# Ten of 31 taps of a convolution on GpSimd, split weights for all products, and later sums

## The chip, the cores and the metric

The kernel runs on one NeuronCore of a Trainium2 chip. The metric is the device time of one execution in microseconds, as a median of runs. TensorE (PE) multiplies matrices, VectorE (DVE) and ScalarE (ACT) do elementwise work, GpSimd (POOL) can do some of it, and SyncE (SP) issues the loads. Each engine works through its own queue in order and waits for the others by semaphores.

## The reference

Two transformer-like blocks run one after the other on x of 256 tokens by 1024 features, in fp32. The first has an attention over compressed, selected and windowed keys, a short convolution of 3 taps, and an FFN. The second, to which most of the change belongs, is in short:

```
n = rmsnorm(h) ;  z = n @ w_in                    # c_a, c_g, q, k, v, qi, ki, wi, two gates
u = c_a * sigmoid(c_g)
u = causal_depthwise_conv(u, conv_w[31, 1024]) + conv_b      # y[t] = sum over d of w[30-d] * u[t-d]
y_conv = silu(layernorm(u)) @ w_conv_out
y_attn = attention(q, k, v, top-64 keys by an index of qi, ki, wi) @ w_attn_out
h = h + (g_conv * y_conv + g_attn * y_attn) @ w_mix_out
h = h + cross_attention(rmsnorm(h), rmsnorm(mem))
h = h + relu(rmsnorm(h) @ w_ff1)**2 @ w_ff2 ;  return rmsnorm(h)
```

## The kernel before, in words

Activations lie with features on the 128 partitions and the 256 tokens along the free dimension, in tiles of four groups of features (128 x 4 x 256, fp32, pool "half", 24 buffers, `H4`); a *half* of the 1024 features is one such tile.

Weights come in *units* of 128 x 2048 (1 MB) by DMA from SyncE, in a fixed order (class `Stream`). ScalarE rounds a unit to `wh` (L125, in two pieces of 1024 columns) and VectorE subtracts to get the rest `wl` (L126). A product is then three matmuls, wh·xh, wh·xl and wl·xh (`mm3`, L261 to L263): a unit of the feature-major form (`Feat`) has 16 products of 256 columns, 48 matmuls; a unit of the token-major form (`Tok`) has 8 of 512 columns, 24 matmuls. `W.next()` keeps the splits two units ahead of the unit in use (`AHEAD` = 3). Four units, `NATIVE` = 81, 85, 89 and 97 of the order, are not split: their raw weights are multiplied with the raw activations `xn` (L290, and L343 in the token-major form), where each product of a feature-major unit stands in the profile as two instructions. Unit 81 is the first of q, 85 of k, 89 of v (token-major), 97 of a gate.

TensorE's queue is in the program's order (`MANUAL`); for the other engines a planner orders the instructions by their place in the program and by readiness. Work that goes beside the products is written as generators in a list `side`; `pump()` lets each take one step, up to its next `yield`. A feature-major unit pumps twice and a token-major one twice or more, so a step is about half a unit of TensorE's time. `drain(g)` runs what is left of g at that place.

The generators that the change touches:

- `norm_side` in `ffn_up`: after 5 steps the squares (ScalarE) and their folds (VectorE), two steps later the column sums on TensorE (`col_stats`, L427), then the scale, by a power on GpSimd (L435).
- `attention2`: the index products, eight rounds of top-8 (L1050, L1051), then eight chunks of attention, each: scores (L1069), softmax, four steps later the transposes (`probs_T`, L1000), one step after these the product with v (`heads_pv`, L1010) into the single buffer of the PSUM pool `pso`, which ScalarE and VectorE then empty (L1015, L1016).
- `conv`: for each half, 31 taps d = 0 to 30, with shifted slices of u added into y. Tap 0 is ScalarE's alone (L1113). Of the others four in five are multiplied by ScalarE into a tile `cp`, four instructions (L1118), and added by VectorE in one (L1119); one in five is done by VectorE alone, in four multiply-adds (L1122). `CONV_RATE` = (5, 4) yields four times in five taps. It starts when the first half of u is ready, and must be done before the product with `w_conv_out`.
- `cross`: the cross attention's four products with v alternate between the PSUM pools `pss` and `pso`.

After the second half of the projections (`group(xs2, ...)`) stand q, k, v and the gates, 20 units, and beside these run `conv` and `attention2`.

Of the kernel before, what the change touches and what calls it, by code (L numbers as in the profile page):

```python
# [9 lines left out]
F32 = mybir.dt.float32  # L10
# [6 lines left out]
T = 256  # L17
# [119 lines left out]

RAW_BUFS = 3
LOAD_AHEAD = 2
NATIVE = (81, 85, 89, 97)  # L140
SPLIT_BUFS = 3
AHEAD = 3
H_BUFS = 24
# [4 lines left out]
LAG2 = 4  # L148
# [10 lines left out]
def hybrid_conformer_kernel(ctx, tc, stop, dbg, xT, memT, wall, wtok, wkiwi, wcmp, par_d, cst_d, gfin_d, out):  # L159
# [105 lines left out]
    class Feat:  # L265
# [7 lines left out]
        def chunk(self, c):  # L273
# [10 lines left out]
            def one(kk, o):  # L284
                k = ks[kk]
                sl = slice(o * 128, o * 128 + 128)
                first = c == 0 and kk == 0 and o % 2 == 0
                last = end and kk == 3
                if wl is None:
                    P.matmul(out=ps[o // 2][:, o % 2].rearrange("p (a s) -> p a s", s=2), lhsT=wh[:, kk, sl], rhs=turns(act.raw(k)), start=first, stop=last, skip_group_check=True)  # L290
                else:
                    mm3(ps[o // 2][:, o % 2], wh[:, kk, sl], wl[:, kk, sl], act.hi(k), act.lo(k), first, last)

# [180 lines left out]
    with tc.manual_schedule(engines=MANUAL):  # L474
# [399 lines left out]
        def ffn_up(act, src, tagr, bcast):  # L874
            res = {}

            def norm_side():
                for _ in range(5):
                    yield
                s = sq_sum(src, "s")  # L880
                yield
                yield
                ps = col_stats(s)
                r = rstd_col(ps, D, "r" + tagr)
                r2 = const.tile([128, 2], F32, name="rsq" + tagr)
                V.tensor_tensor(r2, r, r, op=ALU.mult)
                res["col"] = r2
                if not bcast:
                    return
                dg = col_diag(r2)  # L890
                yield
                ps = diag_bcast(dg)
                rb = S([128, T], "rb", 4)
                A.activation(out=rb, in_=ps, func=AF.Copy)
                res["b"] = rb
# [108 lines left out]

        def heads_pv(pt, nb, v, h0, sp, tt, pool=None):

            po = PS() if pool is pss else pso.tile([128, 512], F32, name="o", tag="o")
            for r in range(2):
                for b in range(nb):
                    P.matmul(out=po[:, r * 128:r * 128 + 128], lhsT=v(b, h0 + r), rhs=pt[:, r, b],  # L1010
                             start=(b == 0), stop=(b == nb - 1))
            tk = slice(tt * 128, tt * 128 + 128)
            o = po[:, 0:256].rearrange("p (r t) -> p r t", r=2)
            h, l = sp.hi(h0, 2)[:, :, tk], sp.lo(h0, 2)[:, :, tk]
            A.activation(out=h, in_=o, func=AF.Copy)  # L1015
            V.tensor_sub(l, o, h.bitcast(F32))  # L1016

        def attention2():
# [39 lines left out]
                yield  # L1058
            chunks = [(tt, hp) for hp in range(4) for tt in range(2)]
            live = {}  # L1060
            for n in range(len(chunks) + LAG2 + 1):
                if n < len(chunks):
                    tt, hp = chunks[n]
                    S_ = 128 * (tt + 1)
# [18 lines left out]
                m = n - LAG2  # L1083
                if 0 <= m < len(chunks):
                    live["t", m] = probs_T(live.pop(m), chunks[m][0] + 1)
                m = n - LAG2 - 1
                if m >= 0:
                    tt, hp = chunks[m]
                    heads_pv(live.pop(("t", m)), tt + 1,
# [14 lines left out]
        def conv():  # L1104
            cnt = 0
            for hf in range(2):
                while ("u", hf) not in done:
                    yield
                for d in range(31):
                    w = [par[:, wco + 8 * (30 - d) + 4 * hf + i:wco + 8 * (30 - d) + 4 * hf + i + 1] for i in range(4)]  # L1110
                    if d == 0:
                        for i in range(4):
# [11 lines left out]
                    cnt += 1  # L1124
                    if cnt * CONV_RATE[1] // CONV_RATE[0] != (cnt - 1) * CONV_RATE[1] // CONV_RATE[0]:
                        yield
                if hf == 0:
                    s = H4(name="ys")
                    V.tensor_tensor(s[:, 0:2], y[0][:, 0:2], y[0][:, 2:4], op=ALU.add)
# [154 lines left out]
        def cross():  # L1284
# [24 lines left out]
                if n == 1:  # L1309
                    yield  # L1310
            for n, (tt, hp) in enumerate(chunks):
                heads_pv(live.pop(("t", n)), 2, lambda b, h: vmf[b][:, 128 * h:128 * h + 128], 2 * hp, cs2, tt, pool=pso if n % 2 else pss)

        cr = start(cross())
        pump()
# [181 lines left out]
```

## Time and profile before

| | us |
|---|---|
| median of 3 runs | 923.16 (922.21 to 924.12) |
| profiled execution | 920.19 |
| its span | 918.1 |
| busy: TensorE, VectorE, ScalarE, GpSimd | 897.3, 658.5, 546.0, 16.9 |

The profile is of one execution. Lines such as L126 are those of the kernel's file; `wl<-wr,wh` are the tile that an instruction writes and those that it reads. Times stand in us from the span's start, means in ns. Matmuls are pipelined, so the time of one (some 0.28 us for 256 columns) is longer than its distance to the next, and the distance between starts is what a product costs.

### The profile page before, as it was taken

The page shows a single profiled execution, that of the slowest core. Times are in us where ns is not written, and L with a number is a line of the kernel's source. Part 1 is how long each engine was busy: PE and PEld are TensorE (multiplying, and loading weights), DVE is VectorE, ACT ScalarE, POOL GpSimd, SP SyncE. Part 2 cuts the span into 40 slices and gives each one's busy share as a digit, 9 for nine tenths or more (in the row PEclk, how much of TensorE's full clock was granted, in tenths as well). Part 3 has the DMA queues.
Part 4 walks back from the last instruction along what each step waited for, and adds up shares of the span by engine and source line. Part 5 has one row for each costly group of instructions (what it writes and reads, how often), then busy time and mean ns, then how long its engine had stood idle before and what let it go on. Part 6 is the DMA issues. An engine that isn't in the chain of part 4 may idle for free.

```text
span 918.1 us, 17258 instructions
## 1 busy us (share of the span) xinstructions
PE 897.3 (98%) x7238; PEld 857.1 (93%) x7238; DVE 658.5 (72%) x1033; ACT 546.0 (59%) x921; POOL 16.9 (2%) x21
## 2 busy tenths in 40 slices
PE   8999999999989999999999999999999999999996
PEld 8999988999989999999998879989999899998885
DVE  5578898458666775548699988987787675675542
ACT  7534667444556664435696799977566565654432
POOL 0011000000000000000000000000000000000000
PEclk9999999999999999999999999999999999999999
DMA  8754533455545565553553445344565263555541
GB/s 310 282 176 145 200 108 127 147 214 191 187 145 206 199 229 198 212 187 139 205 186 107 172 175 197 126 151 178 204 254 184 93 233 140 195 191 198 214 138 46
DMA packets 25998, 165.00 MB, mean 180 GB/s; under 512 B 3008, under 2 KB 3648, under 8 KB 7360
## 3 DMA queue, kind: packets, MB, share of 16 engines
q1 hardware_dynamic: 25632, 163.38, 50.0%
q8 instruction: 56, 0.92, 0.4%
q10 hardware_dynamic: 288, 0.52, 0.1%
q14 instruction: 22, 0.18, 0.1%
HBM read 162.58 MB, written 1.05 MB: 178 GB/s over the span
## 4 chain that ended last, share of the span: by engine, by line
PE 87%; DVE 6%; ACT 3%; issue 2%; DMA 1%; POOL 0%; SPq 0%; POOLq 0%; DVEq 0%
PE m L261 22%; PE m L263 22%; PE m L262 22%; PE m L346 4%; PE m L347 4%; PE m L348 4%; PE m L290 3%; DVE wl L126 3%; ACT wh L125 1%; PE s L721 1%; PE m L343 1%; DVE y L1119 1%; DMA wr<-in_wall_dram 1%; PE o L761 1%; PE o L1010 1%
## 5 line engine op out<-in xcount | busy, mean ns | idle before, releaser
L126 DVE TENSOR_TENSOR wl<-wr,wh 128x1024 fp32r<-128x1024 f32 (+2 forms) x298 | 348.8, 1195 | 163.3 <-ACT wh L125 163.0
L125 ACT ACTIVATE wh<-wr 128x1024 fp32r<-128x1024 f32 (+2 forms) x298 | 298.4, 1036 | 216.2 <-PE m L262 122.2
L261 PE MATMUL m<-xh,wh 128*128 128x256 f32 x384 | 108.8, 283 | 0.4 <-ACT wh L125 0.4
L263 PE MATMUL m<-xh,wl 128*128 128x256 f32 x384 | 105.9, 276 | 0.9 <-DVE wl L126 0.9
L261 PE MATMUL m<-xnh,wh 128*128 128x256 f32 x376 | 106.7, 284 | 0.0
L262 PE MATMUL m<-xh,wh 128*128 128x256 f32 x384 | 105.8, 276 | 0.2 <-DVE xh L401 0.2
L262 PE MATMUL m<-xnh,wh 128*128 128x256 f32 x376 | 103.5, 275 | 0.0
L263 PE MATMUL m<-xnh,wl 128*128 128x256 f32 x376 | 103.5, 275 | 0.0
L1118 ACT ACTIVATE cp<-u,par 128x255 f32<-128x255 f32 (+23 forms) x192 | 78.7, 489 | 0.0
L261 PEld LDWEIGHTS m<-xh,wh 128*128 128x128 f32 x384 | 73.7, 192 | 2.2 <-issue 1.4
L263 PEld LDWEIGHTS m<-xh,wl 128*128 128x128 f32 x384 | 73.8, 192 | 1.3 <-DVE wl L126 1.3
L262 PEld LDWEIGHTS m<-xh,wh 128*128 128x128 f32 x384 | 73.8, 192 | 0.4 <-DVE xh L401 0.4
L262 PEld LDWEIGHTS m<-xnh,wh 128*128 128x128 f32 x376 | 72.2, 192 | 0.8 <-issue 0.5
L261 PEld LDWEIGHTS m<-xnh,wh 128*128 128x128 f32 x376 | 72.2, 192 | 0.8 <-issue 0.5
L263 PEld LDWEIGHTS m<-xnh,wl 128*128 128x128 f32 x376 | 72.3, 192 | 0.0
L261 PE MATMUL m<-x5h,wh 128*128 128x256 f32 x256 | 71.7, 280 | 0.0
L261 PE MATMUL m<-fh,wh 128*128 128x256 f32 x256 | 71.5, 279 | 0.0
L263 PE MATMUL m<-x5h,wl 128*128 128x256 f32 x256 | 71.3, 278 | 0.0
L262 PE MATMUL m<-x5h,wh 128*128 128x256 f32 x256 | 71.2, 278 | 0.0
L263 PE MATMUL m<-fh,wl 128*128 128x256 f32 x256 | 71.2, 278 | 0.0
L262 PE MATMUL m<-fh,wh 128*128 128x256 f32 x256 | 71.2, 278 | 0.0
L261 PE MATMUL m<-hh,wh 128*128 128x256 f32 x256 | 70.6, 276 | 0.0
(364 smaller groups left out, 2327.5 us busy)
## 6 DMA issues: line engine op xcount, KB each, us to landing
wr<-in_wall_dram SPq DMA_DIRECT2D x145, 1024.0 KB, 4.9
wr<-in_wall_dram SPq DMA_DIRECT2D x8, 256.0 KB, 6.2
mem<-in_memT_dram SPq DMA_DIRECT2D x4, 512.0 KB, 6.2
wr<-in_wtok_dram SPq DMA_DIRECT2D x2, 560.0 KB, 5.2
x<-in_xT_dram SPq DMA_DIRECT2D x4, 256.0 KB, 5.5
wr<-in_wall_dram SPq DMA_DIRECT2D x2, 512.0 KB, 7.5
wck<-in_wcmp_dram SPq DMA_DIRECT2D x2, 512.0 KB, 7.3
cst<-in_cst_dram SPq DMA_DIRECT2D x1, 776.0 KB, 8.9
```

The costliest lines, as they stand in the source:

```text
L125: self.nc.scalar.activation(out=hi[:, sl], in_=raw[:, sl], func=AF.Copy)
L126: self.nc.vector.tensor_sub(lo[:, sl], raw[:, sl], hi[:, sl].bitcast(F32))
L261: P.matmul(out=ps_ap, lhsT=wh, rhs=xh, start=first, stop=False, skip_group_check=True)
L262: P.matmul(out=ps_ap, lhsT=wh, rhs=xl, start=False, stop=False, skip_group_check=True)
L263: P.matmul(out=ps_ap, lhsT=wl, rhs=xh, start=False, stop=last, skip_group_check=True)
L290: P.matmul(out=ps[o // 2][:, o % 2].rearrange("p (a s) -> p a s", s=2), lhsT=wh[:, kk, sl], rhs=turns(act.raw(k)), start=first, stop=last, ...
L343: P.matmul(out=o, lhsT=act.raw(k)[:, tk], rhs=wh[:, w], start=first, stop=last)
L346: P.matmul(out=o, lhsT=xh, rhs=wh[:, w], start=first, stop=False)
L347: P.matmul(out=o, lhsT=xh, rhs=wl[:, w], start=False, stop=False)
L348: P.matmul(out=o, lhsT=xl, rhs=wh[:, w], start=False, stop=last)
L721: P.matmul(out=psv[:, :, 0:S_], lhsT=q[:, j, tk], rhs=kz[:, g, :, 0:S_])
L1118: A.activation(out=p[:, i, 0:T - d], in_=u[hf][:, i, 0:T - d], func=AF.Copy, scale=w[i])
```

## The change

`NATIVE` is empty, so each unit is split. In `norm_side` the squares come after 9 steps instead of 5, and the column sums five steps behind them instead of two. In `attention2` the product with v comes two steps behind its transposes instead of one, and in `cross` the four products with v use the pools pss, pso, pss and psm. In `conv` the ten taps d = 1, 4, ..., 28 of each half go to GpSimd: each is four products (`tensor_scalar`) into a tile `gp`, added (`tensor_tensor`) to an accumulator `y2`; the first is written into `y2` itself. All of a half's GpSimd instructions are issued in the program ahead of its other 21 taps, without a step between. The 21 stay as they were, at the same rate, and after the last VectorE adds `y2` to y.

```diff
-NATIVE = (81, 85, 89, 97)
+NATIVE = ()
...
-                    P.matmul(out=ps[o // 2][:, o % 2].rearrange("p (a s) -> p a s", s=2), lhsT=wh[:, kk, sl], rhs=turns(act.raw(k)), start=first, stop=last, skip_group_check=True)
+                    P.matmul(out=plain(ps[o // 2])[:, o % 2], lhsT=wh[:, kk, sl], rhs=v3(act.raw(k)), start=first, stop=last, skip_group_check=True)
...
             def norm_side():
+                for _ in range(9):
+                    yield
+                s = sq_sum(src, "s")
                 for _ in range(5):
                     yield
-                s = sq_sum(src, "s")
-                yield
-                yield
                 ps = col_stats(s)
...
         def heads_pv(pt, nb, v, h0, sp, tt, pool=None):
 
-            po = PS() if pool is pss else pso.tile([128, 512], F32, name="o", tag="o")
+            if pool is psm:
+                po = psm.tile([128, 2, T], F32, name="m", tag="m").rearrange("p a t -> p (a t)")
+            else:
+                po = PS() if pool is pss else pso.tile([128, 512], F32, name="o", tag="o")
...
-            for n in range(len(chunks) + LAG2 + 1):
+            for n in range(len(chunks) + LAG2 + 2):
...
-                m = n - LAG2 - 1
+                m = n - LAG2 - 2
                 if m >= 0:
                     tt, hp = chunks[m]
                     heads_pv(live.pop(("t", m)), tt + 1,
...
             for hf in range(2):
                 while ("u", hf) not in done:
                     yield
-                for d in range(31):
+                y2 = H4(name="y2")
+                for d in range(1, 31, 3):
+                    p = y2 if d == 1 else H4(name="gp")
+                    for i in range(4):
+                        o_ = wco + 8 * (30 - d) + 4 * hf + i
+                        G.tensor_scalar(p[:, i, d:T], u[hf][:, i, 0:T - d], par[:, o_:o_ + 1], None, op0=ALU.mult)
+                    if d > 1:
+                        G.tensor_tensor(y2[:, :, d:T], y2[:, :, d:T], p[:, :, d:T], op=ALU.add)
+                for d in [d for d in range(31) if d % 3 != 1]:
...
                     if cnt * CONV_RATE[1] // CONV_RATE[0] != (cnt - 1) * CONV_RATE[1] // CONV_RATE[0]:
                         yield
+                V.tensor_tensor(y[hf][:, :, 1:T], y[hf][:, :, 1:T], y2[:, :, 1:T], op=ALU.add)
...
-                heads_pv(live.pop(("t", n)), 2, lambda b, h: vmf[b][:, 128 * h:128 * h + 128], 2 * hp, cs2, tt, pool=pso if n % 2 else pss)
+                heads_pv(live.pop(("t", n)), 2, lambda b, h: vmf[b][:, 128 * h:128 * h + 128], 2 * hp, cs2, tt, pool=(pss, pso, pss, psm)[n])
```

## Rows read from the trace of the kernel before

**Rows 1.** The page's part 1: busy time, share of the span and instructions of each engine.

```profile
PE 897.3 (98%) x7238; PEld 857.1 (93%) x7238; DVE 658.5 (72%) x1033; ACT 546.0 (59%) x921; POOL 16.9 (2%) x21
```

**Rows 2.** TensorE's longest waits: who waited for whom, us in total, times, longest.

```profile
PE s L427 <- DVE sq L419: 3.6, 1, 3.6
PE s L427 <- ACT wh L125: 3.6, 1, 3.6
PE o L1010 <- DVE ch L1016: 1.4, 1, 1.4
PE o L1010 <- DVE ah L1016: 1.3, 1, 1.3
```

**Rows 3.** Busy us of PE, PEld, DVE, ACT, POOL by stretch; granted clock, DMA.

```profile
260.00:280.00 20.00, 17.89 (x145) 17.92 (x146) 12.72 (x19) 9.41 (x13) 1.07 (x1) 0.91 0.37 135
```

**Rows 4.** TensorE's timeline behind the first wait: start us, duration us, instruction.

```profile
263.09 0.42 PE L263 MATMUL m<-fh,wl 128*128 128x256 f32 x1
...
265.65 0.42 PE L263 MATMUL m<-fh,wl 128*128 128x256 f32 x1
```

**Rows 5.** TensorE's timeline in running products: feature-major unit, then token-major unit.

```profile
487.02 0.28 PE L263 MATMUL m<-xnh,wl 128*128 128x256 f32 x1
...
489.03 0.28 PE L263 MATMUL m<-xnh,wl 128*128 128x256 f32 x1
...
555.68 0.38 PE L347 MATMUL m<-wl,xnh 128*128 128x512 f32 x1
...
564.32 0.38 PE L348 MATMUL m<-wh,xnh 128*128 128x512 f32 x1
```

**Rows 6.** Busy time by stretch, as in rows 3, while the convolution runs.

```profile
451.40:559.00 107.60, 107.60 (x738) 93.45 (x737) 99.21 (x169) 92.73 (x191) 0.00 (x0) 1.00 0.47 170
...
451.40:616.00 164.60, 163.28 (x1150) 145.03 (x1149) 152.99 (x270) 145.40 (x324) 0.00 (x0) 1.00 0.45 162
```

**Rows 7.** The chain that ended last: start us, us on the chain, native products.

```profile
515.77 8.67 PE m L290 x32
540.52 8.64 PE m L343 x16
```

**Rows 8.** Single lines, 451.4 to 616 or all: ns min/median/max, first and last start.

```profile
L126 DVE TENSOR_TENSOR wl<-wr,wh x43: 684/1216/1224, 451.4 to 614.8; 128x1024 fp32r<-128x1024 f32 x41, 128x512 fp32r<-128x512 f32 x2
...
L1118 ACT ACTIVATE cp<-u,par x192: 472/489/511, 449.5 to 611.8; 128x255 f32<-128x255 f32 x8, 128x254 f32<-128x254 f32 x8, 128x253 f32<-128x253 f32 x8, 128x251 f32<-128x251 f32 x8
...
L1119 DVE TENSOR_TENSOR y<-y,cp x48: 1091/1152/1224, 453.1 to 612.3; 128x1020 f32<-128x1020 f32 x2, 128x1016 f32<-128x1016 f32 x2, 128x1012 f32<-128x1012 f32 x2, 128x1004 f32<-128x1004 f32 x2
...
L1122 DVE SCALAR_TENSOR_TENSOR y<-u,par,y x48: 437/452/472, 459.8 to 609.9; 128x252 f32<-128x252 f32 x8, 128x247 f32<-128x247 f32 x8, 128x242 f32<-128x242 f32 x8, 128x237 f32<-128x237 f32 x8
```

**Rows 9.** Busy time by stretch of L1119 alone, then of L1122 alone.

```profile
451.40:559.00 107.60, 38.45 (x33) 1.00 0.47 170
...
451.40:559.00 107.60, 13.58 (x32) 1.00 0.47 170
```

**Rows 10.** GpSimd's lines: shapes, count, busy us, mean ns, idle before.

```profile
L566 POOL MEMSET kz<- 64x512 f32 x2 | 1.0, 518 | 0.1
...
L1021 POOL MEMSET kid<- 64x256 f32 x2 | 0.7, 327 | 0.1
```

**Rows 11.** GpSimd's timeline: start us, duration us, instruction, idle before it.

```profile
48.08 4.18 POOL L613 TENSOR_TENSOR coqk<-msqk,mhalf 128x24 f32<-128x24 f32 x1 [25.11 <-DVE msqk L611]
71.17 3.81 POOL L669 TENSOR_TENSOR msc<-msc,mhalf 128x16 f32<-128x16 f32 x1 [18.92 <-DVE msc L668]
...
702.84 0.70 POOL L435 TENSOR_TENSOR r<-ms,mhalf 128x2 f32<-128x2 f32 x1 [74.99 <-DVE ms L434]
760.58 1.07 POOL L435 TENSOR_TENSOR rf<-ms,mhalf 128x2 f32<-128x2 f32 x1 [57.05 <-DVE ms L434]
```

**Rows 12.** VectorE's timeline beside two of these.

```profile
71.01 1.21 DVE L126 TENSOR_TENSOR wl<-wr,wh 128x1024 fp32r<-128x1024 f32 x1
...
760.42 0.68 DVE L388 TENSOR_TENSOR hh<-pr,hh 128x512 fp32r<-128x512 f32 x1
```

## The prediction

> **What bounds the kernel now.** I read the busy line first, then the busy time by stretches, then TensorE's waits, and then the VectorE and GpSimd instructions of the convolution. TensorE is busy for 897.3 of the 918.1 us, and GpSimd for 16.9 [rows 1]. The reader is to see that TensorE's queue is the clock of this kernel: an edit gains only what it takes out of that queue or out of its waits, and it costs only where another engine makes TensorE wait. TensorE's largest waits are few: 3.6 us twice at L427 (the column sums of the two FFN norms) and 1.4 and 1.3 us at L1010 (the products with v) [rows 2]. After a 3.6 us wait the clock is low: the stretch 260 to 280 shows a mean of 0.91 [rows 3], and there sixteen matmuls follow each other at 213 ns (from 263.09 to 265.65 in 12 steps) [rows 4], where the running step is 112 ns (487.02 to 489.03 in 18 steps) [rows 5]; that is 1.2 against 2.4 GHz. In the stretch of the 31-tap convolution, 451.4 to 616, VectorE is busy for 153.0 of 164.6 us and up to 559 for 99.2 of 107.6, while TensorE hardly waits [rows 6]. VectorE there is nearly a second bound.
>
> The profiled execution took 920.19 us (span 918.1 and 2.1 around it). The median of the runs, 923.16, lies 3.0 above it; I add the 3.0 at the end.
>
> **The change, part by part.**
>
> *Native products.* A native unit holds TensorE for 8.66 us (two stretches of 16 instructions, 4.33 us each, on the chain) and the token-major one for 8.64 [rows 7]. Split into three products, a unit is 48 steps of 112 ns, 5.36 us, and a token-major one 24 steps of 216 ns (555.68 to 564.32 in 40 steps), 5.18 us [rows 5]. Gain: 3 x 3.30 + 3.46 = **13.4 us** of TensorE, all on the path. In return each unit needs two more splits: 8 x 1.216 = 9.7 us of VectorE [rows 8]. The altered access pattern of the native branch runs in no unit any more: nothing.
>
> *The norm's sums, twice.* The column sums come 5 steps behind the squares instead of 2; a step is half a unit, 2.7 us, so they get some 8 us more against a wait of 3.6. I take both waits as gone, 7.2 us, and with them 15 or so slow steps of 0.1 us each, 3.1 us: **10.3 us**. What is late next is the use of the result, but that is needed only after the eight groups of the FFN (32 steps). Squares and folds are the same instructions, three and a half steps later, where both engines have caught up with the previous evictions; if they have not, a wait of up to the old size stays.
>
> *The later v-products and the third PSUM pool.* The wait of 1.3 us is for the one buffer of that pool to be emptied, the one of 1.4 us the same in the cross attention. A fourth buffer answers the second; one more step of delay gives the first 2.7 us. I take **2.7 us**, between 1 and 2.7. The attention has 14 steps then, and 16 are there before it is drained, so nothing is left over.
>
> These three make 26.4 us, 893.8 of the profiled execution, if nothing else waits.
>
> *The taps.* Of a half's 31 taps ten go: eight that ScalarE multiplied (4 x 0.489 us) and VectorE added (1.152), and two that VectorE did alone (4 x 0.452) [rows 8]. ScalarE loses 31.3 us, VectorE 2 x (9.2 + 3.6) = 25.7. One sum per half of 1.2 us comes back. VectorE's work in the whole stretch is then 153.0 - 25.7 + 9.7 + 2.4 = 139.4 us, TensorE's 163.3 - 13.4 = 149.9: room of 10.5 us. But the pace of the taps stays 1.25 per step. The 42 that are left (32 adds, 8 taps of multiply-adds, and two that ScalarE does alone) are issued in the first 34 steps, to the place that is 559 now, and by then before had done 33 adds and 8 taps of multiply-adds [rows 9]. So up to there VectorE has 99.2 + 7.3 (three units' splits) + 2.4 = 108.9 us, and TensorE 107.6 - 10.1 = 97.5. VectorE lags by 11.4 us; the splits stand two units ahead, 10.7 us, and cover nearly all of it. Without any more, TensorE waits some **3 us** (0 to 11).
>
> *GpSimd's own price.* 80 products of on average 241 columns and 18 sums of 4 x 240. Before shows neither. The nearest rows are two memsets: 512 columns in 518 ns, 256 in 327 [rows 10], which is 0.75 ns a column and 0.14 us fixed. By these a product is 0.32 us and a sum 0.85: 41 us in all, the lower bound. The far other end is the power, 24 columns in 4.18 us [rows 11], 158 ns a column; an add isn't a power, so this end decides nothing. I take the memset rate for products and twice its slope for sums, which read two tensors: 80 x 0.32 + 18 x 1.57 = **54 us**. The Trainium skill, GPSIMD Engine Reference, "Elementwise — side-by-side cycle accounting", gives 4497 ns for a sum of 2048 fp32 columns. An estimate from that page is 2.1 us a sum, 63 us in all and some 8 us on the result; no run here shows it yet.
>
> *VectorE beside GpSimd.* This decides. The same power of two columns takes 0.70 us with VectorE idle (702.84) and 1.07 us at 760.58 [rows 11], where VectorE had begun a two-input sum at 760.42 that ends at 761.10 [rows 12]. The power of 16 columns takes 3.81 us, 0.9 more than 0.38 + 16 x 0.158 us, and it began 0.16 us after a VectorE subtraction of 1.21 us [rows 11, 12]. Each time GpSimd loses what VectorE still has to run, less 0.15. So GpSimd waits for a running two-input instruction of VectorE; whether VectorE waits for a running GpSimd instruction no row shows. The two bounds are nothing and the whole 54 us (a gain is excluded: GpSimd speeds up no VectorE instruction). I take the whole, since what one side shows looks like an either-or, and since nearly all of VectorE's time there is two-input work: splits 43 x 1.216, adds 48 x 1.152, multiply-adds 48 x 0.452, 129 of 153 us, 0.84 [rows 6, 8]. 0.84 x 54 = **45 us** added to VectorE.
> The Trainium skill says just this of the other direction: SBUF — State Buffer, "Who interferes with whom", has an exclusive lock on the second read interface for the whole instruction, so that a VectorE instruction with two SBUF inputs blocks behind a GpSimd one that reads. By that rule the forecast holds; by the rows alone the first rival has as much room as its bound.
>
> Over the whole stretch VectorE then needs 139.4 + 45 = 184.4 us against TensorE's 149.9: at least 34 us of waits. Up to step 34 alone it is 11.4 + 45 - 10.7 = 46. What is late there is the split of the next weights, queued in VectorE's order behind older taps, and TensorE waits for it. I take the middle, **40 us**, the 3 above included: 893.8 + 40 = 933.8, with the 3.0 to the median **937 us**.
>
> **Rivals.**
>
> *Free sharing, faster.* VectorE never waits for GpSimd: 893.8 + 3 + 3.0 = 900 us. For it: VectorE's own durations beside the powers stay as elsewhere (1.21 and 0.68) [rows 12]. Against it: GpSimd's do not. Between nothing (3 us) and 45 us (40 us) the loss grows by 0.82 per us, so it is faster than before while VectorE loses less than 28 us, 0.29 us per GpSimd instruction.
>
> *Half of it.* GpSimd works mostly while VectorE runs one-input work (the top-8 rounds, reductions) or waits for ScalarE: 22 us lost, 21 us of TensorE waits: 918 us, between 908 and 924.
>
> *GpSimd is too slow, and its sum is waited for.* Each half's closing add stands in VectorE's queue 17 steps (46 us at TensorE's pace) behind the half's start, with the next splits queued behind it, and TensorE behind them. At twice my price GpSimd needs 54 us of its own per half besides its waits; VectorE loses 0.84 x 107 = 90 us and TensorE waits some 80: 893.8 + 80 + 3.0 = 977 us, from 955 on. The memset rows speak against it.
>
> *The waits return.* The sums or v-products meet the same wait later, and 22 us are lost beside GpSimd: 893.8 + 10.3 + 21 + 3.0 = 928 us, between 920 and 936.
>
> **How the numbers follow.** Forecast 0.48 (own range 925 to 955), free sharing 0.24 (894 to 908), half 0.15, too slow 0.10, returned waits 0.03. Below 897 and above 960 lie about 0.2, so the range is 897 to 960. A measurement here tells apart about 0.2%, 1.8 us. Faster: 0.24 + 0.13 of the half + 0.01 = 0.38; same: 0.02 each of the half and the forecast, 0.01 of the returned waits = 0.05; slower: 0.46 + 0.10 + 0.01 = 0.57.
>
> **What would show it.** In the profile after: L290 and L343 gone and TensorE's busy time 13 us lower between 451 and 616 than its span there; no wait at L427 and the clock at 1.00 behind it; L1010 without waits. For the port: L126 and L1119 longer than 1.22 us while GpSimd runs, or idle time in front of them; TensorE waiting for L126 by some 40 us between 451 and 600; GpSimd's products 0.3 us and its sums 1.6 us where VectorE pauses. I am wrong if L126 keeps its 1.22 us and TensorE has no waits at L126: then the time is near 900. I am wrong the other way if the closing add of the halves is what VectorE waits for.

## The result, and the profile after

The changed kernel takes 998.29 us (median of 4 runs, 997.1 to 1000.42) against 922.68: 1.0820 times as long, with a 95% interval of 1.0795 to 1.0845. I had forecast 937 and a range up to 960. The direction is right. The time is 61 us off, and lies beyond the rival "GpSimd is too slow, and its sum is waited for" (977), to which I gave one chance in ten.

The profiled execution has a span of 995.2 us. Its page, as in [rows 1], with the 40 slices:

```profile
PE 897.7 (90%) x7294; PEld 866.3 (87%) x7294; DVE 668.2 (67%) x1011; ACT 530.2 (53%) x865; POOL 154.8 (16%) x119
...
PE   8999999999999999996159763698999999999997
...
POOL 0020000000000000019943995000000000000000
PEclk9999999999999999998569975799999999999999
```

TensorE's busy time is that of before, 897.7 against 897.3 us. The 77 us by which the span grew are idle time of one stretch, the nineteenth to the twenty-sixth slice, and there the granted clock falls as well. In stretches, with the columns of [rows 3]:

```profile
240.00:280.00 40.00, 40.00 (x360) 40.00 (x359) 29.32 (x38) 24.47 (x32) 1.07 (x1) 1.00 0.56 193
446.40:640.00 193.60, 111.05 (x767) 103.53 (x765) 128.60 (x178) 98.39 (x195) 135.74 (x97) 0.77 0.27 97
```

The first line, behind the norm's column sums, is what I had hoped for: 40 of 40 us busy and the clock at 1.00, where [rows 3] had a stall and 0.91. The second is the convolution: TensorE works for 111 of 194 us at 0.77, where before it was busy for 163.3 of 164.6 [rows 6]. VectorE is busy for 129 of the 194 us, so it stands still for a third of the time. TensorE's waits, as in [rows 2] (lines shifted: L1013 was L1010, the kid memset L1024 was L1021):

```profile
PE s L1041 <- POOL kid L1024: 32.2, 1, 32.2
PE m L346 <- ACT wh L125: 18.9, 1, 18.9
PE s L1148 <- DVE ys L1145: 9.6, 1, 9.6
PE s L1027 <- ACT rb L1210: 8.6, 1, 8.6
PE m L261 <- ACT q L1217: 6.8, 2, 4.8
PE m L263 <- DVE wl L126: 6.7, 5, 3.8
PE o L1013 <- DVE ah L1019: 2.5, 1, 2.5
```

L427 is gone from this list. What I had expected in its place, some 40 us for wl, is 6.7 us. The rest is mostly new, and four of the five largest, 66.5 us together, lead to GpSimd: kid by its releaser, wh, rb and q by ScalarE's queue, below. L1041 is the index product with kid, L1027 the one that makes kid's contents from rb, and L346 and L261 are products of the projections. The chain that ended last says so too (page, shares of the span): GpSimd has 14% of it now, where the page of before gives it 0%.

```profile
PE 68%; POOL 14%; DVE 7%; issue 5%; ACT 4%; DMA 1%; SPq 0%; POOLq 0%; DVEq 0%; ACTq 0%
```

GpSimd's two lines of the taps (ns: min/median/max), then its timeline at the start and the end of half 0:

```profile
L1117 POOL TENSOR_SCALAR gp<-u,par x72: 846/908/2932, 444.6 to 607.6; 128x252 f32<-128x252 f32 x8, 128x249 f32<-128x249 f32 x8, 128x246 f32<-128x246 f32 x8, 128x243 f32<-128x243 f32 x8
```

```profile
L1119 POOL TENSOR_TENSOR y<-y,gp x18: 2102/2296/2959, 464.3 to 608.6; 128x1008 f32<-128x1008 f32 x2, 128x996 f32<-128x996 f32 x2, 128x984 f32<-128x984 f32 x2, 128x972 f32<-128x972 f32 x2
```

```profile
444.55 0.91 POOL L1117 TENSOR_SCALAR gp<-u,par 128x252 f32<-128x252 f32 x1
446.36 11.62 POOL L1117 TENSOR_SCALAR gp<-u,par 128x252 f32<-128x252 f32 x10
...
464.31 2.30 POOL L1119 TENSOR_TENSOR y<-y,gp 128x1008 f32<-128x1008 f32 x1
...
504.38 2.51 POOL L1117 TENSOR_SCALAR gp<-u,par 128x228 f32<-128x228 f32 x3
506.97 2.10 POOL L1119 TENSOR_TENSOR y<-y,gp 128x912 f32<-128x912 f32 x1
509.13 0.67 POOL L1024 MEMSET kid<- 64x256 f32 x2
```

A product takes 0.91 us at 252 columns and 0.84 at 228 (3 in 2.51 us) where nothing holds it up, 0.87 on average, and 1.16 in the row at 446.36 (10 in 11.62 us); I had 0.32. A sum takes 2.10 us at best, at 912 columns; I had 1.57. The Trainium skill, GPSIMD Engine Reference, "Elementwise — side-by-side cycle accounting", had led to an estimate of 2.1 us a sum, and this trace agrees with it roughly (2.10 at 912 columns, 2.30 at 1008; the estimate was for 960).

The last of these rows is the largest wait of TensorE. The memset of kid, two instructions of 0.67 us together, stands in GpSimd's queue behind all 49 instructions of half 0, and TensorE, which needs kid, stops from 477.6 to 509.85:

```profile
477.30 0.31 PE L263 MATMUL m<-xnh,wl 128*128 128x256 f32 x1
509.85 1.22 PE L1041 MATMUL s<-kid,qi 128*128 128x256 f32 x2 [32.24 <-POOL kid L1024]
```

The second way is through ScalarE. A gp tile is one of the 24 half buffers, from which ScalarE's cp takes too; with GpSimd late, cp waits for a buffer and stands in front of the splits wh and of the evictions rb and q in ScalarE's queue. The largest of ScalarE's waits for GpSimd:

```profile
ACT cp L1129 <- POOL y L1119: 25.8, 7, 5.6
```

The closing adds wait for no result here. GpSimd is done at 611, and the closing add of half 1 starts at 637.32, because the taps in front of it were late; the column sum (L1148, 9.6 us) stands behind it.

### The profile page after: what moved, and what is told of

Same layout as the page of the kernel before. It is cut to its first block, busy times and chain, and to the rows that moved or that the text cites. A ratio compares the mean times of both kernels' runs of the same rounds, so it can differ in the third digit from the quotient of the medians.

```text
span 995.2 us, 17395 instructions
## 1 busy us (share of the span) xinstructions
PE 897.7 (90%) x7294; PEld 866.3 (87%) x7294; DVE 668.2 (67%) x1011; ACT 530.2 (53%) x865; POOL 154.8 (16%) x119
## 4 chain that ended last, share of the span: by engine, by line
PE 68%; POOL 14%; DVE 7%; issue 5%; ACT 4%; DMA 1%; SPq 0%; POOLq 0%; DVEq 0%; ACTq 0%
PE m L261 18%; PE m L262 18%; PE m L263 18%; POOL gp L1117 8%; POOL y L1119 4%; PE m L346 3%; PE m L347 3%; PE m L348 3%; DVE wl L126 3%; ACT wh L125 1%; PE s L721 1%; DVE y L1130 1%; ACT cp L1129 1%; DMA wr<-in_wall_dram 1%; PE o L761 1%
## 5 line engine op out<-in xcount | busy, mean ns | idle before, releaser
L126 DVE TENSOR_TENSOR wl<-wr,wh 128x1024 fp32r<-128x1024 f32 (+2 forms) x306 | 364.0, 1214 | 174.6 <-ACT wh L125 174.2
L125 ACT ACTIVATE wh<-wr 128x1024 fp32r<-128x1024 f32 (+2 forms) x306 | 307.2, 1036 | 249.4 <-PE m L262 143.0
L261 PE MATMUL m<-xnh,wh 128*128 128x256 f32 x424 | 125.1, 295 | 7.3 <-ACT q L1217 6.8
L263 PE MATMUL m<-xnh,wl 128*128 128x256 f32 x424 | 120.7, 285 | 5.8 <-DVE wl L126 5.8
L262 PE MATMUL m<-xnh,wh 128*128 128x256 f32 x424 | 120.6, 284 | 0.0
L261 PE MATMUL m<-xh,wh 128*128 128x256 f32 x384 | 108.8, 283 | 1.0 <-ACT wh L125 1.0
L261 PEld LDWEIGHTS m<-xnh,wh 128*128 128x128 f32 x424 | 85.4, 201 | 9.1 <-ACT q L1217 7.3
L263 PEld LDWEIGHTS m<-xnh,wl 128*128 128x128 f32 x424 | 85.3, 201 | 6.4 <-DVE wl L126 6.4
L1117 POOL TENSOR_SCALAR gp<-u,par 128x252 f32<-128x252 f32 (+8 forms) x72 | 86.7, 1217 | 0.0
L262 PEld LDWEIGHTS m<-xnh,wh 128*128 128x128 f32 x424 | 85.3, 201 | 1.2 <-issue 1.0
L261 PEld LDWEIGHTS m<-xh,wh 128*128 128x128 f32 x384 | 73.6, 192 | 2.8 <-issue 1.4
L261 PE MATMUL m<-x5h,wh 128*128 128x256 f32 x256 | 70.8, 277 | 0.0
L261 PE MATMUL m<-fh,wh 128*128 128x256 f32 x256 | 70.6, 276 | 0.0
L261 PE MATMUL m<-hh,wh 128*128 128x256 f32 x256 | 70.6, 276 | 0.0
L262 PE MATMUL m<-hh,wh 128*128 128x256 f32 x256 | 70.4, 275 | 0.0
L263 PE MATMUL m<-hh,wl 128*128 128x256 f32 x256 | 70.4, 275 | 0.0
```

The source lines that it names most:

```text
L125: self.nc.scalar.activation(out=hi[:, sl], in_=raw[:, sl], func=AF.Copy)
L126: self.nc.vector.tensor_sub(lo[:, sl], raw[:, sl], hi[:, sl].bitcast(F32))
L261: P.matmul(out=ps_ap, lhsT=wh, rhs=xh, start=first, stop=False, skip_group_check=True)
L262: P.matmul(out=ps_ap, lhsT=wh, rhs=xl, start=False, stop=False, skip_group_check=True)
L263: P.matmul(out=ps_ap, lhsT=wl, rhs=xh, start=False, stop=last, skip_group_check=True)
L1117: G.tensor_scalar(p[:, i, d:T], u[hf][:, i, 0:T - d], par[:, o_:o_ + 1], None, op0=ALU.mult)
```

## The experiments

Each ratio is to runs of the kernel before on the same chip. Differences between two changed kernels are differences of their medians; I don't read less than 3 us out of them.

**1 to 3: the queue and the buffers.** My theory after the trace: GpSimd is slow, and kid and the shared buffers make the others wait for it. The rival, called the port theory in the expectations: the loss is the shared reading alone, and the waits are only its places.

e1 moves the memset:
```diff
-G.memset(kid[...], 0.0)
+V.memset(kid[...], 0.0)
```


> The changed kernel with one edit: the two memsets of kid go to VectorE instead of GpSimd, where they stand behind the 49 tap instructions of the first half. Queue theory (GpSimd's order makes TensorE wait at L1041 for 32.2 us): that wait falls below 2 us, and the low clock behind it goes too; if nothing else were late, 998 - 32 - 8 = 958 us. Buffer theory (products of taps hold the H buffers, ScalarE stands behind them and with it the splits): most of the 32 us comes back as waits for L125 or L126, 975 to 990 us. Port theory (VectorE and GpSimd block each other): 990 or more, with waits for L126.

e2 gives gp a tile of its own, two of the four chunks at a time:
```diff
-p = y2 if d == 1 else H4(name="gp")
 for i in range(4):
-    G.tensor_scalar(p[:, i, d:T], u[hf][:, i, 0:T - d], ...)
-if d > 1: G.tensor_tensor(y2[:, :, d:T], y2[:, :, d:T], p[:, :, d:T], op=ALU.add)
+    p = y2[:, i] if d == 1 else gpt[:, i % 2]      # gpt: [128, 2, T], outside the pool
+    G.tensor_scalar(p[:, d:T], u[hf][:, i, 0:T - d], ...)
+    if d > 1 and i % 2:
+        G.tensor_tensor(y2[:, i - 1:i + 1, d:T], y2[:, i - 1:i + 1, d:T], gpt[:, :, d:T], op=ALU.add)
```


> The changed kernel with one edit: GpSimd's products go into a tile of their own of two groups of features (2 KB a partition) instead of H buffers, and each tap has two sums of half the size. Buffer theory: ScalarE's waits for POOL y (25.8 + 5.9 + 4.5 us) fall below 3 us, TensorE's waits for L125 (18.9), q L1217 (6.8) and rb L1210 (8.6) go; kid still waits for the queue, and TensorE comes to it earlier, so the first half gains nothing: 965 to 980 us. Queue theory alone: 995 to 1005 (the same wait at kid, the sums somewhat dearer). Port theory: 995 to 1005, with waits for L126 in place of those.

e3 does both.


> Both edits of the two runs before in one. Queue and buffers together are the cause: TensorE's waits for kid and for ScalarE go; what is left is the closing add that waits for GpSimd, the column sums of the convolution (L1148) and VectorE's lengthening: 920 to 950 us. Port theory: 985 or more.

Measured: e1 994.59 us (1.0783, 1.0751 to 1.0814), e2 994.51 (1.0789, 1.0760 to 1.0819), e3 981.67 (1.0642, 1.0612 to 1.0672). All three are above what my theory gave; e1 lies where the port theory put it (990 or more), e2 at the edge of what that theory and the queue alone both gave (995 to 1005), and e3 close under the port theory's 985. So the times alone don't decide between the two. The traces say more; here are the waits of TensorE and ScalarE in e1, of TensorE in e2, and of TensorE and VectorE in e3:

```profile
PE m L346 <- ACT wh L125: 17.6, 1, 17.6
PE m L261 <- ACT q L1217: 14.4, 2, 10.1
```

```profile
ACT cp L1129 <- POOL y L1119: 48.0, 13, 5.5
```

```profile
PE s L1041 <- POOL kid L1024: 50.3, 1, 50.3
PE s L1150 <- DVE ys L1147: 20.6, 1, 20.6
```

```profile
PE s L1150 <- DVE ys L1147: 38.7, 1, 38.7
PE m L263 <- DVE wl L126: 26.3, 6, 13.4
```

```profile
DVE y L1140 <- POOL y L1121: 35.8, 2, 24.2
```

Without the kid wait ScalarE's waits for buffers grew (cp from 25.8 to 48.0 us); without these the waits for wh at L346, rb and q are gone and the kid wait grew from 32.2 to 50.3. Without both, the closing adds wait 35.8 us for GpSimd, and TensorE 38.7 us for the column sum behind them. So the waits are in series: whichever is taken away, GpSimd is late at the next. What the shared reading costs by itself, e4 measures below.

**4, 6 and 10: what the sharing costs by itself.** In these the kernel before keeps all 31 taps and its native products; GpSimd gets work that nobody waits for, and kid's memset goes to VectorE. e4 has the change's reads, with other operands and into a tile of its own; e6 has as long a stream of writes; e10 has one-input products alone.
```diff
 # per half, ahead of the taps; gpt [128, 2, T] is a tile of its own
+for d in range(1, 31, 3):                                                     # e4
+    for i in range(4):
+        G.tensor_scalar(gpt[:, i % 2, d:T], u[hf][:, i, 0:T - d], par[:, i:i + 1], ...)
+        if d > 1 and i % 2: G.tensor_tensor(gpt[:, :, d:T], gpt[:, :, d:T], cst[...], op=ALU.add)
+G.tensor_scalar(gpt[:, 0], u[hf][:, 0], ...); 110 x G.memset(gpt, 0.0)         # e6
+64 x G.tensor_scalar(gpt[:, d % 2, 0:240], u[hf][:, d % 4, 0:240], ...)        # e10
```


> The kernel before with all its 31 taps on ScalarE and VectorE, kid's memset on VectorE, and a stream on GpSimd that nobody waits for: for each half 40 products that read u and 18 sums of half size, the same amount of reading as the ten taps, into a tile of its own. Port theory as predicted: VectorE loses most of GpSimd's 56 us per half, since it is busy for 93% there: 960 to 1000 us. Half of it: 940 to 960. If queue and buffers are all of the loss and the port costs nothing: 921 to 926.

> The kernel before with the kid memset on VectorE and, in GpSimd's place, per half one product that reads u and 110 memsets of 128x512 on a tile of its own, that nobody waits for (by the 518 ns of such a memset 57 us per half, as long as the taps would take alone). All 31 taps stay on ScalarE and VectorE. It is the fourth run with the reads taken out. Theory 'GpSimd's reads and VectorE's exclude each other': writes alone cost VectorE nothing, 921 to 926 us. Theory 'any GpSimd instruction holds VectorE up': about as the reading stream, 940 to 955.

> The kernel before with the kid memset on VectorE and, on GpSimd, 64 one-input products of 240 columns per half that nobody waits for (0.87 us each where VectorE pauses, 56 us per half, as much GpSimd time as the idle stream of the fourth run; no two-input sums). Theory 'any read by GpSimd excludes VectorE': as the fourth run, 945 to 955. Theory 'only GpSimd's two-input sums do': 922 to 930.

Measured: e4 951.59 us (1.0319, 1.0292 to 1.0346), e6 922.72 (1.0007, 0.9993 to 1.0021), e10 930.40 (1.0092, 1.0069 to 1.0114). So e4 gives the "half of it" of the port theory. Here are the busy times of all engines in e4 and in e10, and then GpSimd's lines and two of VectorE's between 446 and 640 (busy us, mean ns), of e4, e10 and e6:

```profile
PE 910.3 (96%) x7238; PEld 867.9 (91%) x7238; DVE 694.7 (73%) x1035; ACT 546.7 (58%) x921; POOL 199.3 (21%) x135
```

```profile
PE 902.0 (97%) x7238; PEld 860.8 (93%) x7238; DVE 669.4 (72%) x1035; ACT 546.1 (59%) x921; POOL 202.9 (22%) x147
```

```profile
L1113 POOL TENSOR_SCALAR gpt<-u,par 128x255 f32<-128x255 f32 (+9 forms) x80 | 123.6, 1555 | 31.5 <-DVE u L219 27.7
L1115 POOL TENSOR_TENSOR gpt<-gpt,cst 128x504 f32<-128x504 f32 (+8 forms) x36 | 59.4, 1650 | 3.0
```

```profile
L126 DVE TENSOR_TENSOR wl<-wr,wh 128x1024 fp32r<-128x1024 f32 (+1 forms) x45 | 60.0, 1350 | 3.3 <-ACT wh L125 3.3
...
L1129 DVE SCALAR_TENSOR_TENSOR y<-u,par,y 128x252 f32<-128x252 f32 (+5 forms) x44 | 26.9, 645 | 0.0
```

```profile
L1112 POOL TENSOR_SCALAR gpt<-u,par 128x240 f32<-128x240 f32 x128 | 186.7, 1474 | 30.4 <-DVE u L219 27.8
```

```profile
L126 DVE TENSOR_TENSOR wl<-wr,wh 128x1024 fp32r<-128x1024 f32 (+1 forms) x48 | 58.7, 1239 | 3.4 <-ACT wh L125 3.4
...
L1126 DVE SCALAR_TENSOR_TENSOR y<-u,par,y 128x252 f32<-128x252 f32 (+5 forms) x48 | 23.5, 526 | 0.0
```

```profile
L1113 POOL MEMSET gpt<- 128x512 f32 x220 | 116.1, 528 | 12.6
```

```profile
L126 DVE TENSOR_TENSOR wl<-wr,wh 128x1024 fp32r<-128x1024 f32 (+1 forms) x52 | 61.3, 1197 | 5.8 <-ACT wh L125 5.8
...
L1127 DVE SCALAR_TENSOR_TENSOR y<-u,par,y 128x252 f32<-128x252 f32 (+5 forms) x48 | 20.2, 460 | 0.0
```

Beside writes VectorE keeps its times (multiply-adds 460 ns, splits 1197). Beside reads both lose. VectorE's busy time over the whole span is 694.7 us in e4, 669.4 in e10 and 658.5 before: 36.2 and 10.9 us lost, of which 0.5 each is kid's memset on VectorE. By e10 a product costs VectorE 10.9 / 128 = 0.085 us, while it waits 0.6 us itself (1.474 against the 0.87 of a free one). If it costs the same in e4, its 36 sums of two inputs cost (36.2 - 80 x 0.085) / 36 = 0.82 us each, of the 1.14 that one lasts at least (in e3). That is an estimate: no run has the sums alone. So the theory of e10 that any read excludes VectorE is wrong in size, and that only the two-input sums do is nearly right by the time (930.40 against 922 to 930). The time follows VectorE's loss: 28.7 us for 36.2, 8.1 for 10.9, 0.8 and 0.74 per us.

**5, 9, 17 and 18: a later place for the result.** e5 is e3 with a step after every tap and, in the program, both closing adds 50 steps behind the start, where the taps ended before; e9 is the change with that alone; e17 is e5 with 20 steps in place of 8; e18 is e5 with the two adds held at that place in VectorE's queue.
```diff
-CONV_RATE = (5, 4)
+CONV_RATE = (1, 1)
-V.tensor_tensor(y[hf][:, :, 1:T], y[hf][:, :, 1:T], y2[:, :, 1:T], op=ALU.add)   # at the end of each half
+ya.append(y2)
+if hf == 1:
+    for _ in range(8): yield                                                     # e17: 20
+    for h_ in range(2): V.tensor_tensor(y[h_][:, :, 1:T], ..., ya[h_][:, :, 1:T], op=ALU.add)
+                        # e18: tc.keep_in_program_order(V.tensor_tensor(...))
```


> The changed kernel with the kid memset on VectorE and a gp tile of its own (two half-size sums per tap), and GpSimd's results wanted later: one step after each of the 21 remaining taps (42 steps instead of 33), both closing adds moved behind the second half's taps and 8 further steps, 50 steps in all as the 62 taps had before. GpSimd still does all its taps. Theory 'GpSimd is the bound and its sum is waited for': GpSimd ran without pause from 445.5 to 620 us in the last run, so with 17 more steps the 38.7 us wait of the column sum and the 35.8 us wait of the closing adds go, and only the shared port is left: 940 to 955 us. Theory 'the sharing itself is the whole loss': TensorE's waits for the ScalarE and VectorE splits stay and grow, 970 to 985.

> The changed kernel with only the delay of the fifth run: a step after each remaining tap, closing adds and column sum behind the second half's taps and 8 more steps, 50 steps in all. The kid memset stays on GpSimd and the gp tiles stay in the pool that ScalarE's cp also takes from. Theory 'three separate waits for GpSimd's queue (kid, the shared tiles, the result)': only the third goes, the kid wait of 32 us stays or grows and ScalarE still stands behind gp tiles: 975 to 990. Theory 'the place of the result is the whole of it': 950 to 960, as with all three removed.

> The fifth run with 20 in place of 8 steps between the second half's last tap and the closing adds, 62 steps in all; 10 taps per half on GpSimd. Theory 'the result was still the larger part': the 18.1 us wait at the second closing add shrinks or goes, 935 to 948, less what the later end of the convolution costs (about 13 us for 12 steps without GpSimd taps). Theory 'the shared reading is the 38.7 us': nothing is won, and the later end is added: 955 to 967.

> The fifth run (8 steps before the closing adds, 50 in all, 10 taps per half on GpSimd) with the two closing adds kept at their place in the program's order, where the planner had drawn them forward. Theory 'what was left in the fifth run is mostly the wait for GpSimd's result': VectorE's 10.2 and 18.1 us waits go or shrink to a few us, 918 to 932 (by the 6 taps' 4.2 us above none, scaled with GpSimd's work, 922). Theory 'with 10 taps the shared reading itself costs some 30 us or more, as in the idle stream': 943 to 955.

Measured: e5 953.70 us (1.0336, 1.0315 to 1.0357), e9 968.15 (1.0491, 1.0466 to 1.0515), e17 972.71 (1.0548, 1.0519 to 1.0577), e18 937.66 (1.0155, 1.0136 to 1.0175). e9 keeps its kid wait (38.4 us), as the theory of three waits had it, and is still 30 us faster than the change, below the 975 to 990 of that theory and above the 950 to 960 of the other: the pace and the place of the result, which e9 and e5 change together, are the largest of the three, and not the whole. e17 lies above both of its theories (935 to 948, 955 to 967).

e5 came out where I expected it, and I took it at first for the price of the sharing. Its trace speaks against that. VectorE's closing adds of e5, then of e17, then of e18, and what VectorE waited for in front of them:

```profile
541.12 1.22 DVE L1146 TENSOR_TENSOR y<-y,y 128x1020 f32<-128x1020 f32 x1 [10.20 <-POOL y L1122]
...
627.92 1.22 DVE L1146 TENSOR_TENSOR y<-y,y 128x1020 f32<-128x1020 f32 x1 [18.09 <-POOL y L1122]
```

```profile
541.60 1.22 DVE L1146 TENSOR_TENSOR y<-y,y 128x1020 f32<-128x1020 f32 x1 [10.19 <-POOL y L1122]
...
628.33 1.22 DVE L1146 TENSOR_TENSOR y<-y,y 128x1020 f32<-128x1020 f32 x1 [18.04 <-POOL y L1122]
```

```profile
629.90 1.21 DVE L1146 TENSOR_TENSOR y<-y,y 128x1020 f32<-128x1020 f32 x1
...
636.03 1.22 DVE L1146 TENSOR_TENSOR y<-y,y 128x1020 f32<-128x1020 f32 x1 [4.92 <-POOL y L1122]
```

The planner of the kernel had drawn the adds forward to the same two places, 12 steps later in the program or not, and VectorE stood 10.2 and 18.1 us before them. With the adds held 4.9 us are left, and the time falls by 16 us. TensorE's largest waits of e18:

```profile
PE m L263 <- DVE wl L126: 10.4, 8, 5.1
PE s L1154 <- DVE ys L1151: 8.6, 1, 8.6
```

So both theories of e18 miss by some 5 us (932 and 943 are the ends that face it). Without the last 8.6 us wait for the column sum, ten taps on GpSimd would cost some 14 us against none (937.66 - 8.6 - 915.05); that is worked out, not run.

**7, 8, 12 to 14: the other three edits.** e12 has the later norm sums alone, e7 these and the v-products, e8 all of the change without the GpSimd taps, e13 the norm sums and no natives, e14 as e13 with a step after each of the 62 taps.
```diff
+norm sums as in the change                          # e12, e7, e8, e13, e14
+v-products as in the change                         # e7, e8
-NATIVE = (81, 85, 89, 97)
+NATIVE = ()                                         # e8, e13, e14
-CONV_RATE = (5, 4)
+CONV_RATE = (1, 1)                                  # e14
```


> The kernel before with only the norm sums later and the v-products one step later and on three accumulators; the native products and all 31 taps stay. Theory 'these terms were sized rightly' (10.3 and 2.7 us): 908 to 912 us. Theory 'the waits return elsewhere': 918 to 924.

> The changed kernel without the GpSimd taps (all 31 taps on ScalarE and VectorE, no second accumulator): natives off, norm sums and v-products as changed. Theory 'the native term is 13.4 us besides the 13 of the others': 894 to 899 us. Theory 'the split pieces that the former native products now need cost VectorE and ScalarE what TensorE saves': 905 to 915.

> The kernel before with only the norms' column sums later (5 steps behind the squares, and the squares 9 steps on). By my step 10.3 us: 911 to 914. If the v-products bring their 2.7 us in the seventh run, this one is 2.7 us slower than that run (913.75), 916 to 917; if they bring nothing, it is equal to it within 1.5 us.

> The kernel before with the norms' sums later and the native products off; v-products and all 31 taps as before, 62 taps in 50 steps. Against the norms' sums alone (911.93): theory 'VectorE, at the pace of the taps, takes back what TensorE gains': 910 to 915. Theory 'it was the later v-products that took it': the natives bring most of their 13.4 us, 899 to 904.

> The same with a step after every tap, 62 taps in 62 steps in place of 50, so that VectorE has fewer taps between two splits. Theory 'it is the pace': TensorE's waits for wl and ah go, 899 to 905. Theory 'the convolution's end is the bound': the column sum comes 12 steps later and what needs it waits, 912 or more.

Measured: e12 911.93 us (0.9885, 0.9865 to 0.9906), e7 913.75 (0.9902, 0.9879 to 0.9925), e8 915.05 (0.9921, 0.9901 to 0.9941), e13 911.57 (0.9873, 0.9851 to 0.9895), e14 924.33 (1.0019, 1.0005 to 1.0033). The norm sums are worth 10.4 us. e7 lies between its theories (908 to 912, 918 to 924). The v-products bring nothing: the waits at L1013 are 3.2 us in e7, those at L1010 were 2.7 in e12. The natives bring nothing either, with the v-products or without. TensorE's busy time falls by 9.7 us from e12 to e13 (895.9 to 886.2), and its waits take that back. Those of e13, then of e14:

```profile
PE o L1010 <- DVE ah L1016: 6.1, 1, 6.1
PE m L263 <- DVE wl L126: 4.4, 5, 2.3
```

```profile
PE m L261 <- ACT sh L390: 7.3, 1, 7.3
PE s L1136 <- DVE ys L1133: 6.9, 1, 6.9
PE s L427 <- DVE sq L419: 6.0, 1, 6.0
...
PE o L1010 <- DVE ah L1016: 1.6, 1, 1.6
...
PE m L263 <- DVE wl L126: 1.1, 3, 0.6
```

At a slower pace the waits for wl and ah go (4.4 to 1.1, 6.1 to 1.6), and the column sum and what needs it come too late (6.9, 7.3 and 6.0 us). The time is what the theory of the convolution's end gave (912 or more); the waits show that the other had part of it: the pace is behind those for wl and ah, and the end of the convolution leaves no room to slow it.

**11, 15 and 16: a smaller share.** e11 is e3 with 4 taps of each half on GpSimd in place of 10; e15 spreads the 54 others over 50 steps instead of 43; e16 has 6 taps on GpSimd and 50 steps.
```diff
-for d in range(1, 31, 3):
+for d in range(1, 31, 8):                           # e11, e15; e16: 5
-CONV_RATE = (5, 4)
+CONV_RATE = (27, 25)                                # e15; e16: (1, 1)
```


> The changed kernel with 4 taps per half on GpSimd instead of 10 (1, 9, 17, 25), the kid memset on VectorE and a gp tile of its own; the closing adds where the change has them. GpSimd's own work is 32 products x 0.87 + 12 half sums x 1.15 = 42 us in place of 111, so its result is there long before it is wanted. Theory 'the loss follows the GpSimd time, and VectorE's relief does not pay for it': 915 without taps + 38.7 x 42/111 = 930, 922 to 935. Theory 'VectorE is the bound without natives, so a small share pays': 900 to 912.

> The run with 4 taps per half on GpSimd, its 54 other taps spread over 50 steps instead of 43. Theory 'the 27 us were the pace of the taps': 912 to 922. Theory 'the shared port is the loss': 935 or more.

> As the fourth-tap run with the 50 steps (917.62), with 6 taps per half on GpSimd (1, 6, 11, ..., 26) in place of 4: 48 products and 20 half sums, 65 us of GpSimd's own work in place of 42, a step after each of the 50 other taps, closing adds at the end of each half. Theory 'most of the 38.7 us was still the result waited for, the shared reading costs a few us': 915 to 923, no wait of VectorE for y2. Theory 'the shared reading grows with GpSimd's time': 915 + 38.7 x 65/111 = 938, 930 to 942.

Measured: e11 942.05 us (1.0213, 1.0195 to 1.0232), e15 917.62 (0.9939, 0.9917 to 0.9962), e16 919.26 (0.9953, 0.9937 to 0.9968). e11 misses both of its theories: fewer taps passed at the old rate press VectorE's other work into fewer steps, and that costs 24 us of the 27 lost against e8. With the 50 steps of before, 8 or 12 of the 62 taps on GpSimd are 2.6 and 4.2 us slower than none, which is hardly more than I read out of such a difference. In e16 VectorE never waits for y2. The share takes 12 adds of 1.152 us from VectorE, 13.8 us, and the reads and the two closing adds (2.4) give back more than that: its busy time is 678.6 us against 667.4 in e8.

The fastest versions are e12 and e13, at 911.9 and 911.6 us: the norm sums alone, natives on or off. None with taps on GpSimd reaches them.

## Why the prediction was wrong

The way from 922.33 to 998.29, each step the difference of two medians above:

| step of the prediction | forecast, us | measured, us | from |
|---|---|---|---|
| later norm sums | -10.3 | -10.4 | before to e12 |
| later v-products | -2.7 | +1.8 | e12 to e7 |
| natives | -13.4 | +1.3 (-0.4 alone) | e7 to e8 (e12 to e13) |
| taps on GpSimd, VectorE held up | +40 (3 of it the pace) | +22.6 | e8 to e18 (8.6 of it the column sum) |
| taps on GpSimd, results waited for, with the old pace | 0 | +60.6 | e18 to the change |

**The step that failed is "GpSimd's own price".** I took "the memset rate for products and twice its slope for sums", 54 us. The free pieces measured are 80 x 0.87 + 18 x 2.1 = 107 us, twice that, and with GpSimd's waits for VectorE 137.9 us (154.8 less the 16.9 of before). Most of the gap is the products, 80 x 0.55 = 44 us; the sums make 10. GpSimd's own waits for VectorE, some 30 us here, I put at nothing, though [rows 11, 12] had shown just that direction. With a small share GpSimd's results are not waited for: e11 and e16, with 42 and 65 us of GpSimd's own work, show no wait of VectorE for y2. At 138 us GpSimd is on the critical chain for 14% of the span, and the step from e18 to the change, 60.6 us that the forecast didn't have, is by the trace mainly its lateness: in the change 66.5 us of TensorE's waits lead to it. I had the right mechanism among the rivals, with the condition "at twice my price", and held it down with "the memset rows speak against it". They don't: a memset reads nothing, and e6 shows that it costs VectorE nothing either. The row that I took as the nearest was of another kind of instruction.

**The old pace has a part in that.** e18 has the 42 taps in 42 steps, the change in 33. I had priced the old pace at 3 us (0 to 11). With four taps of each half on GpSimd it costs 24 us (e11 against e15). With ten taps no run changes the pace alone, so its share of the 60.6 stays open.

**Two ways of that wait I didn't see at all.** I named only the closing add as what waits for GpSimd. The largest wait was a 0.67 us memset of another step, queued on GpSimd behind 49 tap instructions; it was among my rows, as a price, and I didn't ask what stands in front of it now. The other is the pool that gp and cp share. Neither alone is worth more than 4 us (e1, e2), since GpSimd is late for the next as well; both are 16.6 (e3), with the slower pace and the later place 44.6 (e5), with the adds held 60.6 (e18).

**The sharing was priced too high.** The forecast was 40 us of TensorE wait from 45 us on VectorE: 0.84 us lost per us of GpSimd work, 54 us of it. In e4 VectorE lost 36.2 us to some 111 us of GpSimd work (80 x 0.87 + 36 x 1.14), 0.33 per us, and in e18 as much: its busy time is 679.6 us, where e8's 667.4 less the taps taken away (25.7) and with the closing adds (2.4) would be 644.1. A price twice too low and a loss 2.5 times too high partly cancel, which is luck: 22.6 against 40. The slope from VectorE's loss to time, 0.82, was right (0.8 in e4). That e18 takes the 937 us that I had forecast for the change is a coincidence: it has other terms and none of the change's waits for GpSimd.
The rule that I cited from the Trainium skill, SBUF — State Buffer, "Who interferes with whom", holds here in its direction and in its exception: VectorE loses time to GpSimd instructions that read (e4), none to ones that write (e6). In size e10 differs: beside one-input products VectorE lost 0.085 us of 0.87 each, not the whole instruction.

**The natives failed on VectorE.** I had counted their 9.7 us of splits per unit, but against a room that the taps' departure was to make. e13 has no such relief, and in the change the relief was lost to GpSimd. TensorE's gain is there in e13, 9.7 us of busy time of the 13.4, and turns into waits for ah and wl. In the change it doesn't show (897.7 against 897.3): in e8, without the taps, TensorE is busy for 887.3 us, and in the change's stretch at a clock of 0.77 products take longer (L261 with xnh 295 ns in the mean of the span, 284 before).

**The v-products.** The wait in the cross attention fell from 1.4 to 0.4 us by the third accumulator, as I said. The step of delay gave the other nothing (1.3 in e12, 3.2 in e7): what ends it is VectorE's emptying of the buffer, and not the distance. That the taps in VectorE's queue delay this, e13 and e14 suggest (6.1 us, and 1.6 with the taps spread over more steps).

**What was right.** TensorE's queue as the clock of the kernel; both L427 waits and the clock behind them (10.3 forecast, 10.4 measured); VectorE as the second bound; and the sign by which I would be wrong upwards, a VectorE that waits at the closing add, though e3 (35.8 us) and e5 show it and not the change, where kid and the buffers come first. Of the signs for the sharing, the longer L126 came: 1339 ns in the mean between 446 and 640, 1195 before. TensorE's 40 us of waits for it did not (6.7).

## What to carry to other kernels

Before work goes to an engine that was idle, list what already stands in its queue behind the new place, and which pools its tiles come from: TensorE waited 32 us here for a memset of 0.67 us that was last in line, and moving it alone gained only 4, since other waits stood behind it. Price an operation by a row that reads as many inputs as it does, and when the price is unknown within a factor of two, work out at either price whether the result is there when it is wanted. When work is taken away from a loop that is paced by count, the pace has to be set again (e11 and e15: 24 us). Where a planner orders a queue, look up in the trace where it put the instruction that you moved (e5, e17 and e18).

## What the runs showed of the hardware that I had not expected

GpSimd's time per column is another for each kind: 512 columns of memset in 0.53 us, 252 columns of product in 0.91, 912 columns of sum in 2.10. VectorE loses nothing while GpSimd only writes (220 memsets; VectorE busy for 659.9 us, 658.5 before); a one-input product costs VectorE 0.085 us and waits 0.6 itself; a two-input sum of 1.14 us costs VectorE an estimated 0.82, by e4 and e10 together. Why sums cost VectorE so much more than products, no run here shows.
